# Expert weights in 8 KB rows with ordered features, a twentieth place by shared buffers, and the token gather over four PSUM banks

## The chip, the cores and the metric

The kernel runs on one core of one Trainium2 chip, in one launch. The metric is the device time of one execution in microseconds. Before the change it is 1816.79 us, the median of three runs (1816.61 to 1819.65).

## The reference

Everything is computed in fp32. A sequence of 256 tokens of width 1024 (with 16 meta tokens ahead of it in the first part) passes two layers of a first block and then one hybrid layer, whose second half is a mixture of experts. Cut to what matters here:

```
def swiglu(x, w_gate, w_up, w_down):
    return (silu(x @ w_gate) * (x @ w_up)) @ w_down

def first_block(...):                      # 272 x 1024, two layers
    h = h + 0.5 * swiglu(rmsnorm(h), ...)  # inner width 2816
    proj = rmsnorm(h) @ w_in               # retention and differential attention
    h = h + concat([y_ret, y_diff]) @ w_out
    h = h + 0.5 * swiglu(rmsnorm(h), ...)

def hybrid_layer(...):                     # 256 x 1024, modulated by c
    x = x + g1 * (concat([chunk_mlp, attention, hgrn]) @ w_out)
    h2 = rms(x) * norm2_w * (1.0 + sc2) + sh2
    x = x + g2 * hier_moe(h2, ...)

def hier_moe(h, ...):                      # 4 groups of 8 experts, 32 in all
    grp = argmax(h @ w_grp + b_grp)        # each token: one group,
    top_val, top_idx = top_k(e_in, 2)      # then the best 2 of its 8 experts
    gate = softmax(top_val) * p_grp
    out[e] = (silu(xb @ w1[e]) * (xb @ w3[e])) @ w2[e]     # inner width 512
    y = segment_sum(out * gate, token)
```

## The kernel before

The first block and the hybrid layer's mixer take the first 1317 us of the span. The rest is the mixture of experts: a routing stage (`route`), then 16 pairs of experts, one after the other (`pairs`), which begin at about 1336 us. The change lies in these two, but for one small addition in the stage that computes the modulation.

The routing stage normalizes the tokens, computes the logits, picks group and experts, and numbers the tokens of each expert (`place`). Its ACT writes `h2`, the tokens scaled by their norm, with the tokens on the partitions (L1636).

A pair works on 64 slots for each of its two experts, 128 columns in all. Its steps are:

- `picked` (DVE, L1726): two 0/1 matrices `pick` that say which token sits in which slot.
- `tokens`, the gather: for each of the 8 chunks k of 128 features, two matmuls `xgp` (L1738, one for each half of the tokens) of `h2` with `pick`; then an eviction `xg` that applies the norm's weight and the modulation, for even k by ACT (L1744), for odd k by DVE (L1742). The PSUM tiles alternate between the tags "tp" and "po", one bank each.
- `first` (L1767): `ph` = 32 matmuls with the first weight, into one bank, then 32 with the third into another. Each has 64 slots of one expert as the stationary side and 512 columns of the weight as the moving one.
- Silu by ACT (L1508) of the first `ph` into `h`; the product with the second `ph` by DVE (L1512).
- `turned` (four transposes `hTp`, L1773) and `turned_out`, in which ACT copies one half of `hTp` (L1779) and DVE the other (L1780) to `hTe`.
- `last` (L1787): `py`, one tile of two banks (tag "sc"), 16 matmuls for columns 0 to 511 and 16 for 512 to 1023. Behind each half `weighed` follows: `y` = gate x modulation x `py` (DVE, L1795), `yh` = `y` rounded to the matmul's format (ACT, L1796), `yl` = the rest (DVE, L1797).
- `combine`: `po` (L1805, four matmuls per half) adds the pair's result to the tokens' rows, `xtok` (DVE, L1807). It is done one pair later, between the steps of the next pair. `slots` (`pgt`, L1751 and L1755) prepares the transposed matrix and the gates for it.

The program's order on TensorE is written out by hand in this phase (each matmul is pinned behind the one before): the 64 `ph` of pair g, the gather of pair g+1, `hTp` of pair g, `po` of pair g-1, `py`, and so on. The other engines' order follows from a scheduler. Waits are set by tiles: an instruction that writes a tile waits for the earlier readers of that tile's buffer.

After pair 6 the program asks whether an expert has more than 64 tokens (`overflow`, L1561); the results so far are added first, without other work between. The branch is not taken with these inputs.

Weights come by SP's queue (`load`, L1822), in pieces of 1 MB, 12 for a pair: per expert two of the first weight, two of the third (each 512 rows) and two of the second (each 512 columns). A piece has 128 partitions with four rows of 512 values each, so 2 KB lie together in DRAM. The pieces go round a ring of 19 places, most of which are buffers that earlier stages no longer need; MW = 2 of them are the expert phase's own. A piece is fetched as soon as the matmuls of the piece that held its place are done. The last pair's pieces come in smaller parts.

Of the kernel before, what the change touches and what calls it, by code (L numbers as in the profile page):

```python
# [18 lines left out]
P = 128  # L19
D = 1024  # L20
# [126 lines left out]

CUTS = {True: ((0, 256, 512), (0, 256, 512)), False: ((0, 512), (0, 512))}
ORD = (((0, 1, 6, 7),), ((2, 3), (4,), (5,)))
OVERFLOW = 7  # L150
MW = 2
CONSTS = [
# [14 lines left out]
def _pf_layout():  # L167
    o = 0
    for name, n in (("f1n0", 8), ("f1n1", 8), ("mxn0", 8), ("mxn1", 8), ("f2n0", 8), ("f2n1", 8),
                    ("fin", 8), ("n1w", 8), ("gn0", 4), ("gn1", 4), ("sub0", 1), ("sub1", 1),  # L170
                    ("c", 8), ("cctx", 8), ("hgw", 1), ("n2w", 8)):
        PF[name] = (o, n)
        o += n
    return o
# [5 lines left out]
class Kernel:  # L180
# [633 lines left out]
    def modulation(self):  # L814
# [6 lines left out]
        self.mcol = self.cp.tile([P, 4, KC], F32, name="mcol")  # L821
        self.m2col = self.cp.tile([P, 2, KC], F32, name="m2col")
        self.mrow = self.dp.tile([8, 1, D], F32, name="mrow")
        for part in range(6):
# [17 lines left out]
            for i in range(1 + both):  # L842
                hl = self.gp.tile([P, 2, D], F32R, name="mhl", tag="gb")
                for q in range(0, D, 256):
                    qs = slice(q, q + 256)
                    nc.scalar.activation(hl[:, 0, qs], acc[:, i, qs], AF.Copy)
                    nc.gpsimd.tensor_tensor(hl[:, 1, qs], acc[:, i, qs], hl[:, 0, qs].bitcast(F32), op=ALU.subtract)
                    if q % 512:
                        yield
                yield  # L850
                yield
                row = acc[0:1, i]
                for h in range(2):
# [6 lines left out]
                nc.scalar.dma_start(mrow, row)  # L860
                if part not in (2, 5):
# [12 lines left out]
        o = PF["n2w"][0]  # L874
        nc.vector.scalar_tensor_tensor(self.rc, self.rc, 1.0, self.pf[:, o:o + KC], op0=ALU.add, op1=ALU.mult)
        cst = self.cp.tile([P, 64 + 36 + P], F32, name="cst")
        nc.scalar.dma_start(cst, A["rcst"])
# [609 lines left out]
    def pairs(self):  # L1487
# [9 lines left out]
        for g in range(NPAIR):  # L1497
# [48 lines left out]
            for n in range(2):  # L1546
                for c in (slice(a, b) for a, b in zip(CUTS[True][n], CUTS[True][n][1:])):
                    self.last(py, hT, ws[4 + n], cur, n, c)
                    due.append(slice(512 * n + c.start, 512 * n + c.stop))
# [4 lines left out]
    def overflow(self):  # L1554
# [6 lines left out]
        with tc.If(nc.values_load(self.most[0:1, 0:1], min_val=0, max_val=SEQ) > CAP,  # L1561
                   preferred_fallthrough_block=False):
            with tc.For_i(0, NPAIR, 1) as iv:
# [3 lines left out]
                for r in range(1, SEQ // CAP):  # L1567
# [6 lines left out]
                    w = self.weights(src, ring, eng=nc.gpsimd)  # L1574
                    h = self.late.tile([P, 512], F32, name="h", tag="h", bufs=1)
                    for i in range(2):
# [3 lines left out]
                        if i:  # L1580
                            nc.vector.tensor_tensor(h, h, ps, op=ALU.mult)
                        else:
                            nc.scalar.activation(h, ps, AF.Silu)
                    hT = self.turned_out(self.turned(h))
                    self.outputs(cur)
                    py = self.ps.tile([P, 2, 512], F32, name="py", tag="sc", bufs=1)
                    for n in range(2):
                        self.last(py, hT, next(w), cur, n, slice(0, 512))
                        self.combine(cur, slice(512 * n, 512 * n + 512))
# [5 lines left out]
    def route(self):  # L1595
# [3 lines left out]

        before = ep.tile([P, P], F32R, name="before")  # L1600
        nc.vector.tensor_copy(before, self.before)
# [3 lines left out]
        for tt in range(2):  # L1605
            xT = sm.tile([P, KC, P], F32, name="x2T", tag="xg", bufs=2)
            for q in range(2):
# [26 lines left out]
        for tt in range(2):  # L1634
            r = ss[:, tt, 4:5]
            nc.scalar.activation(self.h2[:, tt], self.xtok[:, tt], AF.Copy, scale=r)  # L1636
        cnt = [0]

        def t(*dims):
            cnt[0] += 1  # L1640
            return sm.tile([P, 2] + list(dims), F32, name="r%d" % cnt[0], tag="r%d" % cnt[0], bufs=1)

# [71 lines left out]
    def picked(self, e0, r=0, place=None, room=None):  # L1714

        nc, sm = self.nc, self.sm
        if place is None:
            place = self.place[:, :, e0:e0 + 2]
        pick = sm.tile([P, 2, P], F32, name="pick", tag="pick", bufs=2) if room is None else room[:, KC:]
        for tt in range(2):  # L1720
            pl = place[:, tt]
            if r:
# [5 lines left out]
                                    self.iota[:, None, :].to_broadcast([P, 2, CAP]), op=ALU.is_equal)  # L1728
        xg = sm.tile([P, KC, P], F32, name="xg", tag="xg", bufs=2) if room is None else room
        return {"pick": pick, "xg": xg}  # L1730

    def tokens(self, cur, ks):

        nc = self.nc
        for k in ks:
            ps = self.pbank("xgp", ("tp", "po")[k % 2])
            for tt in range(2):
                self.pin(nc.tensor.matmul(ps[:, :P], self.h2[:, tt, k * P:k * P + P], cur["pick"][:, tt],  # L1738
                                          start=tt == 0, stop=tt == 1))
            o, sc, sh = cur["xg"][:, k], self.rc[:, k:k + 1], self.sh2[:, k:k + 1]  # L1740
            if k % 2:
# [21 lines left out]
    def first(self, ps, cur, w, kk):  # L1763
        for k in range(4):
            for j in range(2):
                hj = slice(CAP * j, CAP * j + CAP)
                self.pin(self.nc.tensor.matmul(ps[hj], cur["xg"][:, 4 * kk + k, hj], w[j][:, k], start=kk + k == 0,  # L1767
                                               stop=kk == 1 and k == 3))

    def turned(self, h):  # L1770
        pt = self.pbank("hTp", "ot")
        for f in range(4):
            self.pin(self.nc.tensor.transpose(pt[:, f * P:(f + 1) * P], h[:, f * P:(f + 1) * P], self.ident))  # L1773
        return pt
# [7 lines left out]

    def last(self, py, hT, w, cur, n, c):
# [4 lines left out]
        self.weighed(py, cur, n, c)  # L1788
# [22 lines left out]

    def load(self, aps, ring, row, col, rows=(0, 4), cols=(0, 512), eng=None):

        ws = []
        for ap in aps:
            pool, tag, bufs = ring.pop(0)
            ring.append((pool, tag, bufs))
            ws.append(pool.tile([P, 4, 512], F32, name="ew", tag=tag, bufs=bufs))
        for k0, k1 in zip(rows, rows[1:]):
            for a, b in zip(cols, cols[1:]):  # L1820
                for w, ap in zip(ws, aps):
                    (eng or self.nc.sync).dma_start(w[:, k0:k1, a:b], ap[row + k0 * P:row + k1 * P, col + a:col + b]  # L1822
                                                    .rearrange("(k p) f -> p k f", p=P))
        return ws

    def weights(self, src, ring, end=False, eng=None):

        for i in range(2):
            for kk in range(2):
                yield self.load([s[i] for s in src], ring, kk * 512, 0, (0, 2, 4) if end else (0, 4), eng=eng)  # L1830
        for n in range(2):
            yield self.load([s[2] for s in src], ring, 0, n * 512, cols=CUTS[end][n], eng=eng)

# [12 lines left out]
def host_arrays(inputs):  # L1846
# [4 lines left out]
    for n in ("ffn1_w_gate", "ffn1_w_up", "ffn1_w_down", "w_in", "w_out", "ffn2_w_gate", "ffn2_w_up",  # L1851
# [7 lines left out]
             "hgw": np.concatenate([g["hgrn_norm_w_2"][0], g["hgrn_norm_w_2"][0]]), "n2w": g["norm2_w_2"][0]}  # L1859
    f["pf"] = np.concatenate([cols(parts[n]) for n in PF], axis=1)  # L1860
    lv = np.stack([g["diff_lambda_q1"], g["diff_lambda_q2"], g["diff_lambda_k1"], g["diff_lambda_k2"]], axis=1)
# [29 lines left out]
```

## Time and profile before

| | us |
|---|---|
| median of three runs | 1816.79 |
| lowest, highest | 1816.61, 1819.65 |
| the profiled execution's own time | 1815.69 |
| its span, first to last instruction | 1814.0 |
| TensorE busy | 1757.8 (97%) |
| DVE busy, ACT busy | 1035.4, 737.1 |

The profile is of one execution, 1.7 us longer than its span and 1.1 us shorter than the median. Engines are PE (TensorE), PEld (its weight loads, which overlap with matmuls), DVE, ACT, POOL and SP, whose queue (SPq) issues transfers. A row of a timeline gives start, duration, engine, line and operation, "out<-in" by the names of the program, the partitions x elements, and in brackets how long the engine stood idle before it and what ended that. Lines (L1738) are those of the kernel before.

### The profile page before, as it was taken

How to read it: one execution, taken by the hardware profiler on the slowest of the kernel's cores; microseconds unless marked ns; L12 is line 12 of the kernel's file. 1: busy time of each engine (PE TensorE's matmuls, PEld its weight loads, DVE VectorE, ACT ScalarE, POOL GpSimd, SP SyncE). 2: the span in 40 equal slices, each digit the busy share in tenths (PEclk: the TensorE clock that was granted, in tenths of full speed). 3: DMA queues.
4: the chain of work that ended last, by engine and by line, in shares of the span. 5: the costliest groups of instructions: out<-in, count | busy, mean ns of one | idle time of the engine just before them, and what ended most of it. 6: DMA issues, size and time to landing. Idle time of an engine off the chain costs nothing. (4 is left out here: it accounts for less than half of the span.)

```text
span 1814.0 us, 30657 instructions
## 1 busy us (share of the span) xinstructions
PE 1757.8 (97%) x12435; PEld 1439.5 (79%) x12435; DVE 1035.4 (57%) x1764; ACT 737.1 (41%) x1312; POOL 343.8 (19%) x341
## 2 busy tenths in 40 slices
PE   9999999999999999999999999999989999899998
PEld 8999988899999999999899999986654444344444
DVE  6875887676667667668677755648332323122323
ACT  6444445454444544444455544656421111111111
POOL 3231273121221213236131102311000000000000
PEclk9999999999999999999999999999989999899999
DMA  8766643255677576754355655431789999999998
GB/s 253 231 209 192 227 163 117 70 171 166 206 232 247 174 249 211 232 189 133 114 172 170 187 190 164 160 123 41 248 315 380 397 400 400 397 400 400 399 398 306
DMA packets 312946, 427.75 MB, mean 236 GB/s; under 512 B 15056, under 2 KB 207312, under 8 KB 312672
## 3 DMA queue, kind: packets, MB, share of 16 engines
q1 hardware_dynamic: 294640, 394.51, 63.1%
q10 hardware_dynamic: 18160, 31.23, 5.2%
q8 instruction: 100, 1.64, 0.4%
q14 instruction: 46, 0.38, 0.1%
HBM read 424.56 MB, written 1.15 MB: 235 GB/s over the span
## 5 line engine op out<-in xcount | busy, mean ns | idle before, releaser
L265 DVE TENSOR_TENSOR whl<-raw,whl 128x1024 fp32r<-128x1024 f32 (+2 forms) x374 | 464.4, 1246 | 208.5 <-ACT whl L264 207.5
L264 ACT ACTIVATE whl<-raw 128x1024 fp32r<-128x1024 f32 (+2 forms) x374 | 383.8, 1032 | 331.2 <-PE pd L275 107.9
L273 PE MATMUL pgu<-xh,whl 128*128 128x272 f32 (+1 forms) x1408 | 403.8, 287 | 3.6 <-DVE g L348 3.3
L275 PE MATMUL pgu<-xh,whl 128*128 128x272 f32 (+1 forms) x1408 | 403.1, 286 | 2.4 <-DVE whl L265 2.4
L274 PE MATMUL pgu<-xl,whl 128*128 128x272 f32 (+1 forms) x1408 | 402.9, 286 | 1.4 <-DVE xl L286 1.4
L273 PEld LDWEIGHTS pgu<-xh,whl 128*128 128x128 f32 x1408 | 264.1, 188 | 5.5 <-issue 3.5
L275 PEld LDWEIGHTS pgu<-xh,whl 128*128 128x128 f32 x1408 | 265.0, 188 | 3.2 <-DVE whl L265 3.0
L274 PEld LDWEIGHTS pgu<-xl,whl 128*128 128x128 f32 x1408 | 265.1, 188 | 2.3 <-DVE xl L286 2.0
L1767 PE MATMUL ph<-ew,xg 128*64 128x512 f32 x1024 | 225.4, 597 | 6.8 <-issue 6.8
L275 PE MATMUL pd<-ah,whl 128*128 128x272 f32 (+1 forms) x704 | 203.2, 289 | 0.3 <-DVE whl L265 0.3
L274 PE MATMUL pd<-al,whl 128*128 128x272 f32 (+1 forms) x704 | 202.4, 288 | 0.0
L273 PE MATMUL pd<-ah,whl 128*128 128x272 f32 (+1 forms) x704 | 202.3, 287 | 0.0
L1767 PEld LDWEIGHTS ph<-ew,xg 128*64 128x64 f32 x1024 | 74.1, 138 | 152.0 <-issue 148.3
L352 POOL TENSOR_TENSOR u<-u,g 128x272 f32<-128x272 f32 (+1 forms) x88 | 92.1, 1047 | 397.1 <-DVE u L351 339.9
L273 PEld LDWEIGHTS pd<-ah,whl 128*128 128x128 f32 x704 | 132.9, 189 | 0.5 <-issue 0.2
L273 PE MATMUL pj<-xh,whl 128*128 128x272 f32 x448 | 133.2, 298 | 0.0
L275 PEld LDWEIGHTS pd<-ah,whl 128*128 128x128 f32 x704 | 132.5, 188 | 0.6 <-DVE whl L265 0.5
L274 PEld LDWEIGHTS pd<-al,whl 128*128 128x128 f32 x704 | 132.8, 189 | 0.1
L274 PE MATMUL pj<-xl,whl 128*128 128x272 f32 x448 | 130.5, 291 | 0.5 <-DVE xl L286 0.5
L275 PE MATMUL pj<-xh,whl 128*128 128x272 f32 x448 | 130.1, 290 | 0.0
L1787 PE MATMUL py<-ew,hTe 128*64 128x512 f32 (+1 forms) x544 | 117.4, 573 | 2.1 <-ACT hTe L1779 1.0
L1512 DVE TENSOR_TENSOR h<-h,ph 128x512 f32<-128x512 f32 x16 | 11.0, 687 | 175.6 <-PE ph L1767 175.6
(442 smaller groups left out, 2733.2 us busy)
## 6 DMA issues: line engine op xcount, KB each, us to landing
ew<-in_w_dram SPq DMA_DIRECT2D x180, 1024.0 KB, 13.8
raw<-in_ffn_w_gate_dram SPq DMA_DIRECT2D x43, 1024.0 KB, 5.5
raw<-in_ffn_w_up_dram SPq DMA_DIRECT2D x43, 1024.0 KB, 5.6
raw<-in_w_in_dram SPq DMA_DIRECT2D x38, 1024.0 KB, 5.1
raw<-in_ffn_w_down_dram SPq DMA_DIRECT2D x32, 1024.0 KB, 6.2
mraw<-in_w_mod_dram ACTq DMA_DIRECT2D x24, 1024.0 KB, 6.0
raw<-in_ffn_w_down_dram SPq DMA_DIRECT2D x16, 768.0 KB, 5.4
ew<-in_w_dram SPq DMA_DIRECT2D x24, 512.0 KB, 11.0
```

The costliest lines, as they stand in the source:

```text
L264: nc.scalar.activation(w[:, 0], part, AF.Copy)
L265: nc.vector.tensor_tensor(w[:, 1], part, w[:, 0].bitcast(F32), op=ALU.subtract)
L273: nc.tensor.matmul(out, wh, xh, start=first, stop=False)
L274: nc.tensor.matmul(out, wh, xl, start=False, stop=False)
L275: nc.tensor.matmul(out, wl, xh, start=False, stop=last)
L352: nc.gpsimd.tensor_tensor(u[:, :N], u[:, :N], g[:, :N], op=ALU.mult)
L1512: self.nc.vector.tensor_tensor(h, h, ph, op=ALU.mult)
L1767: self.pin(self.nc.tensor.matmul(ps[hj], cur["xg"][:, 4 * kk + k, hj], w[j][:, k], start=kk + k == 0, stop=kk == 1 and k == 3))
L1787: self.pin(self.nc.tensor.matmul(py[hj, n, c], hT[:, k, hj], w[j][:, k, c], start=k == 0, stop=k == 3))
```

## The change

Four things are done. (a) A piece is laid so that a partition holds consecutive rows of the weight: 4 rows of 512 values of the first and third weight, or 2 rows of 1024 values of the second, 8 KB in one stretch. Rows p*8+k of the first two now lie on partition p, so the features are gathered in that order: `h2` is written permuted (ACT, with a stride on both sides), the norm's weight and modulation are loaded a second time in that order (`n2e`, `m2e`), Silu writes `h` permuted (`by_row`) and the product reads `ph` with a stride of four values. (b) The ring gets a twentieth place (MW = 3). `pick` and `xg` have one buffer each where they had two, `y` shares the buffer of `h`, and the temporaries of the routing stage use buffers that the expert phase needs later. (c) As a piece of the second weight now has 256 inner rows and all 1024 columns, `last` does the first two inner chunks for both halves of `py`, then the other two; both `weighed` follow behind. The last pair keeps the old way (`last_part`). (d) The gather uses four banks: chunks with k % 4 below 2 a tile `ps` of two banks under the tag "sc" (which `py` uses as well), the others "tp" and "po".

```
-MW = 2
+MW = 3
...
-            h = self.late.tile([P, 512], F32, name="h", tag="h", bufs=1)
-            self.nc.scalar.activation(h, ph, AF.Silu)
+            h = self.late.tile([P, 4, P], F32, name="h", tag="h", bufs=1)
+            self.nc.scalar.activation(self.by_row(h), ph, AF.Silu)
...
-            self.nc.vector.tensor_tensor(h, h, ph, op=ALU.mult)
+            self.nc.vector.tensor_tensor(h, h, ph.rearrange("p (q k) -> p k q", k=4), op=ALU.mult)
...
-                self.last(py, hT, ws[4], cur, 0, slice(0, 512))
+                self.last(py, hT, ws[4], 0)
...
-                self.last(py, hT, ws[5], cur, 1, slice(0, 512))
+                self.last(py, hT, ws[5], 1)
+                for n in range(2):
+                    self.weighed(py, cur, n, slice(0, 512))
...
-            self.nc.scalar.activation(self.h2[:, tt], self.xtok[:, tt], AF.Copy, scale=r)
+            self.nc.scalar.activation(self.h2[:, tt].rearrange("p (k q) -> p k q", k=KC),
+                                 self.xtok[:, tt].rearrange("p (q k) -> p k q", k=KC), AF.Copy, scale=r)
...
-        pick = sm.tile([P, 2, P], F32, name="pick", tag="pick", bufs=2) if room is None else room[:, KC:]
+        pick = sm.tile([P, 2, P], F32, name="pick", tag="pick", bufs=1) if room is None else room[:, KC:]
...
-        xg = sm.tile([P, KC, P], F32, name="xg", tag="xg", bufs=2) if room is None else room
+        xg = sm.tile([P, KC, P], F32, name="xg", tag="xg", bufs=1) if room is None else room
...
     def tokens(self, cur, ks):
+        if "ps" not in cur:
+            cur["ps"] = self.ps.tile([P, 2, 512], F32, name="xgp", tag="sc", bufs=1)
         for k in ks:
-            ps = self.pbank("xgp", ("tp", "po")[k % 2])
+            ps = cur["ps"][:, k % 4, :] if k % 4 < 2 else self.pbank("xgp", ("tp", "po")[k % 2])
...
-            o, sc, sh = cur["xg"][:, k], self.rc[:, k:k + 1], self.sh2[:, k:k + 1]
+            o, sc, sh = cur["xg"][:, k], self.rce[:, k:k + 1], self.she[:, k:k + 1]
...
+    def last(self, py, hT, w, kk):
+        for k in range(2):
+            for n in range(2):
+                for j in range(2):
+                    hj = slice(CAP * j, CAP * j + CAP)
+                    self.pin(self.nc.tensor.matmul(py[hj, n], hT[:, 2 * kk + k, hj], w[j][:, k, n * 512:n * 512 + 512],
+                                                   start=2 * kk + k == 0, stop=2 * kk + k == 3))
...
-        y = self.late.tile([P, 512], F32, name="y", tag="y", bufs=1)[:, :c.stop - c.start]
+        y = self.late.tile([P, 512], F32, name="y", tag="h", bufs=1)[:, :c.stop - c.start]
...
+        for r, c in cuts:
+            for w, ap in zip(ws, aps):
+                ap = ap.rearrange("(p k) f -> p k f", p=P)
+                (eng or self.nc.sync).dma_start(w[:, r, c], ap[:, rows, cols][:, r, c])
```

The two engines of the gather, as the built programs have them. First TensorE (PE), the gather between two pairs, before; "waits Activation_49" is a wait for ACT's semaphore, "waits DVE_49" for DVE's, and a row with xN stands for N alike:

```order
L1738 MATMUL xgp<-pick,h_14530 128x128 x4
L1738 MATMUL xgp<-pick,h_14530 128x128 [waits Activation_49]
L1738 MATMUL xgp<-pick,h_14530 128x128
L1738 MATMUL xgp<-pick,h_14530 128x128 [waits DVE_49]
L1738 MATMUL xgp<-pick,h_14530 128x128
L1738 MATMUL xgp<-pick,h_14530 128x128 [waits Activation_49]
```

The same place on TensorE now, the whole gather with what stands ahead of and behind it (two matmuls are a chunk):

```order
L1787 MATMUL ph_15030<-ew,xg 64x512 x6
L1758 MATMUL xgp<-pick,h_14534 128x128 [waits DVE_49,PE_49]
L1758 MATMUL xgp<-pick,h_14534 128x128
L1758 MATMUL xgp<-pick,h_14534 128x128 [waits Activation_49]
L1758 MATMUL xgp<-pick,h_14534 128x128 x5
L1758 MATMUL xgp<-pick,h_14534 128x128 [waits DVE_49]
L1758 MATMUL xgp<-pick,h_14534 128x128
L1758 MATMUL xgp<-pick,h_14534 128x128 [waits Activation_49]
L1758 MATMUL xgp<-pick,h_14534 128x128 x3
L1758 MATMUL xgp<-pick,h_14534 128x128 [waits DVE_49]
L1758 MATMUL xgp<-pick,h_14534 128x128
L1797 MATMUL hTp<-ident,h 128x128 x4
```

Before, every chunk from the third on waits for the eviction of two chunks ahead. Now chunk 1 (third matmul) and chunk 5 wait for ACT, chunks 4 and 7 for DVE, and chunks 2, 3 and 6 have no wait of their own.

DVE at the overflow check, from the last pair ahead of it to the branch, before:

```order
L1807 TENSOR_TENSOR xtok<-xtok,po 128x512 [waits PE_49] x2
L1795 SCALAR_TENSOR_TENSOR y<-py,gs,g2row 128x512 [waits DVE_49,PE_49]
L1807 TENSOR_TENSOR xtok<-xtok,po 128x512 [waits PE_49] x2
L1797 TENSOR_TENSOR yl<-y,yh 128x512 [waits Activation_49]
L1795 SCALAR_TENSOR_TENSOR y<-py,gs,g2row 128x512 [waits DVE_49,PE_49]
L1807 TENSOR_TENSOR xtok<-xtok,po 128x512 [waits PE_49] x2
```

And now, with the load of the check's value:

```order
L1840 TENSOR_TENSOR xtok<-xtok,po 128x512 [waits PE_49] x4
L1828 SCALAR_TENSOR_TENSOR y<-py,gs,g2row 128x512 [waits DVE_49,PE_49]
L1830 TENSOR_TENSOR yl<-y,yh 128x512 [waits Activation_49]
L1828 SCALAR_TENSOR_TENSOR y<-py,gs,g2row 128x512 [waits DVE_49]
L1840 TENSOR_TENSOR xtok<-xtok,po 128x512 [waits PE_49] x2
L1830 TENSOR_TENSOR yl<-y,yh 128x512 [waits Activation_49]
L1571 TENSOR_LOAD mi [waits DVE_49]
```

The first `y` and its `yl` have moved behind the last `py`, next to the second `y`; two `xtok` additions stand between the second `y` and its `yl`, in both.

## Rows read from the trace of the kernel before

**Rows 1.** The head of the page: span; busy time of the engines.

```profile
span 1814.0 us, 30657 instructions
PE 1757.8 (97%) x12435; PEld 1439.5 (79%) x12435; DVE 1035.4 (57%) x1764; ACT 737.1 (41%) x1312; POOL 343.8 (19%) x341
```

**Rows 2.** A stretch of one pair: busy us by engine, clock, DMA share, GB/s.

```profile
1395.95:1424.65 28.70, 28.39 (x152) 12.81 (x150) 8.33 (x16) 4.52 (x10) 0.00 (x0) 1.00 1.05 403
```

**Rows 3.** The chain of waits through one pair: start, duration, what.

```profile
1609.34 13.73 PE ph L1767 x64
1623.07 0.66 PE xgp L1738 x4
...
1623.75 0.47 ACT xg L1744
...
1624.26 0.73 PE xgp L1738 x4
...
1638.06 13.73 PE ph L1767 x64
```

**Rows 4.** Waits of the weight loads, expert phase: total us, times, longest.

```profile
PEld xgp L1738 <- ACT xg L1744: 13.3, 45, 0.4
...
PEld ph L1767 <- DMA ew<-in_w_dram: 3.4, 12, 0.3
```

**Rows 5.** The timeline of one gather.

```profile
1409.78 0.97 PEld L1738 LDWEIGHTS xgp<-pick,h 128*128 128x128 f32 x8 [0.81 <-issue]
...
1410.00 0.69 DVE L1512 TENSOR_TENSOR h<-h,ph 128x512 f32<-128x512 f32 x1 [11.60 <-PE ph L1767]
1410.54 0.46 ACT L1744 ACTIVATE xg<-xgp,m2col 128x128 f32<-128x128 f32 x1 [6.88 <-PE xgp L1738]
...
1411.04 0.97 PEld L1738 LDWEIGHTS xgp<-pick,h 128*128 128x128 f32 x8 [0.29 <-ACT xg L1744]
1411.80 0.46 ACT L1744 ACTIVATE xg<-xgp,m2col 128x128 f32<-128x128 f32 x1 [0.80 <-PE xgp L1738]
...
1412.30 0.97 PEld L1738 LDWEIGHTS xgp<-pick,h 128*128 128x128 f32 x8 [0.29 <-ACT xg L1744]
...
1413.56 0.97 PEld L1738 LDWEIGHTS xgp<-pick,h 128*128 128x128 f32 x8 [0.29 <-ACT xg L1744]
...
1414.45 0.47 PEld L1773 LDWEIGHTS hTp<-ident,h 128*128 128x128 f32 x4
```

**Rows 6.** Who waited for the two copies of `hTp`: us, times.

```profile
  DVE hTe L1780: 7.5, 15
```

**Rows 7.** The timeline from the last `py` half of pair 6 to the check.

```profile
1535.57 0.20 PEld L1787 LDWEIGHTS py<-ew,hTe 128*64 128x64 f32 x4 [0.36 <-DVE y L1795]
...
1539.30 0.75 DVE L1795 SCALAR_TENSOR_TENSOR y<-py,gs,g2row 128x512 f32<-128x512 f32 x1 [2.16 <-PE py L1787]
...
1539.96 1.27 DVE L1807 TENSOR_TENSOR xtok<-xtok,po 128x512 f32<-128x512 f32 x2
...
1542.46 0.40 PE L1805 MATMUL po<-yl,pT 128*128 128x512 f32 x1
```

**Rows 8.** The timeline from a second `y` to the next Silu.

```profile
1424.90 0.75 DVE L1795 SCALAR_TENSOR_TENSOR y<-py,gs,g2row 128x512 f32<-128x512 f32 x1 [2.21 <-PE py L1787]
...
1426.41 0.69 DVE L1797 TENSOR_TENSOR yl<-y,yh 128x512 fp32r<-128x512 f32 x1 [0.76 <-ACT yh L1796]
...
1431.77 0.60 ACT L1508 ACTIVATE h<-ph 128x512 f32<-128x512 f32 x1 [5.39 <-PE ph L1767]
```

**Rows 9.** DMA queue of SP, 1400:1500 us: packets, MB, share of 16 engines.

```profile
q1 hardware_dynamic: 20034, 39.78, 104.6%
```

**Rows 10.** The same queue in 1133.4:1137.1 us, a load with 8 KB rows.

```profile
q1 hardware_dynamic: 144, 1.05, 82.4%
```

**Rows 11.** ACT's timeline in the routing stage, at `h2`.

```profile
1323.35 2.17 ACT L1636 ACTIVATE h<-xtok,ss 128x1024 f32<-128x1024 f32 x2
1327.60 0.21 ACT L1688 ACTIVATE r<-r 128x8 f32<-128x8 f32 x1 [2.08 <-POOL r L1687]
```

More of the change, by code (lines that the diff above doesn't have):

```diff
@@ L146 @@
 CAP = 64
-CUTS = {True: ((0, 256, 512), (0, 256, 512)), False: ((0, 512), (0, 512))}
+CUTS = ((0, 256, 512), (0, 256, 512))
 ORD = (((0, 1, 6, 7),), ((2, 3), (4,), (5,)))
 OVERFLOW = 7
-MW = 2
+MW = 3
 CONSTS = [
@@ L822, in modulation @@
         self.m2col = self.cp.tile([P, 2, KC], F32, name="m2col")
+        self.m2e = self.cp.tile([P, 2, KC], F32, name="m2e")
         self.mrow = self.dp.tile([8, 1, D], F32, name="mrow")
@@ L860, in modulation @@
                 nc.scalar.dma_start(mrow, row)
+                if part in (3, 4):
+                    nc.scalar.dma_start(self.m2e[:, part - 3], mrow.rearrange("o (p k) -> p (o k)", p=P))
                 if part not in (2, 5):
@@ L1546, in pairs @@
             for n in range(2):
-                for c in (slice(a, b) for a, b in zip(CUTS[True][n], CUTS[True][n][1:])):
-                    self.last(py, hT, ws[4 + n], cur, n, c)
+                for c in (slice(a, b) for a, b in zip(CUTS[n], CUTS[n][1:])):
+                    self.last_part(py, hT, ws[4 + n], n, c)
+                    self.weighed(py, cur, n, c)
                     due.append(slice(512 * n + c.start, 512 * n + c.stop))
@@ L1574, in overflow @@
                     w = self.weights(src, ring, eng=nc.gpsimd)
-                    h = self.late.tile([P, 512], F32, name="h", tag="h", bufs=1)
+                    h = self.late.tile([P, 4, P], F32, name="h", tag="h", bufs=1)
                     for i in range(2):
@@ L1580, in overflow @@
                         if i:
-                            nc.vector.tensor_tensor(h, h, ps, op=ALU.mult)
+                            nc.vector.tensor_tensor(h, h, ps.rearrange("p (q k) -> p k q", k=4), op=ALU.mult)
                         else:
-                            nc.scalar.activation(h, ps, AF.Silu)
+                            nc.scalar.activation(self.by_row(h), ps, AF.Silu)
                     hT = self.turned_out(self.turned(h))
@@ L1587, in overflow @@
                     for n in range(2):
-                        self.last(py, hT, next(w), cur, n, slice(0, 512))
+                        self.last(py, hT, next(w), n)
+                    for n in range(2):
+                        self.weighed(py, cur, n, slice(0, 512))
                         self.combine(cur, slice(512 * n, 512 * n + 512))
@@ L1598, in route @@
         rev = self.rev
-        before = ep.tile([P, P], F32R, name="before")
+        before = self.late.tile([P, P], F32R, name="before", tag="hTe", bufs=1)
         nc.vector.tensor_copy(before, self.before)
@@ L1605, in route @@
         for tt in range(2):
-            xT = sm.tile([P, KC, P], F32, name="x2T", tag="xg", bufs=2)
+            pool, tag = ((sm, "xg"), (self.late, "yh"))[tt]
+            xT = pool.tile([P, KC, P], F32, name="x2T", tag=tag, bufs=1)
             for q in range(2):
@@ L1635, in route @@
             r = ss[:, tt, 4:5]
-            nc.scalar.activation(self.h2[:, tt], self.xtok[:, tt], AF.Copy, scale=r)
-        cnt = [0]
+            nc.scalar.activation(self.h2[:, tt].rearrange("p (k q) -> p k q", k=KC),
+                                 self.xtok[:, tt].rearrange("p (q k) -> p k q", k=KC), AF.Copy, scale=r)
+        room = self.late.tile([P, 1024], F32, name="rt", tag="yl", bufs=1)
+        at = [0]
         def t(*dims):
-            cnt[0] += 1
-            return sm.tile([P, 2] + list(dims), F32, name="r%d" % cnt[0], tag="r%d" % cnt[0], bufs=1)
+            n = 2 * int(np.prod(dims))
+            at[0] += n
+            r = room[:, at[0] - n:at[0]]
+            return r.rearrange("p (a b c) -> p a b c", a=2, b=dims[0]) if len(dims) > 1 else r.rearrange("p (a b) -> p a b", a=2)
         tt_, pool = nc.vector.tensor_tensor, nc.gpsimd.tensor_tensor
@@ L1768, in first, with by_row @@
                                                stop=kk == 1 and k == 3))
+    def by_row(self, h):
+        return h.rearrange("p k q -> p q k")
     def turned(self, h):
@@ L1781, in turned_out, with last_part @@
         return hT
-    def last(self, py, hT, w, cur, n, c):
+    def last(self, py, hT, w, kk):
+        for k in range(2):
+            for n in range(2):
+                for j in range(2):
+                    hj = slice(CAP * j, CAP * j + CAP)
+                    self.pin(self.nc.tensor.matmul(py[hj, n], hT[:, 2 * kk + k, hj], w[j][:, k, n * 512:n * 512 + 512],
+                                                   start=2 * kk + k == 0, stop=2 * kk + k == 3))
+    def last_part(self, py, hT, w, n, c):
         for k in range(4):
@@ L1810, in combine, with load @@
                 eng.dma_start(self.A["out"][0, tt * P:(tt + 1) * P, ns], self.xtok[:, tt, ns])
-    def load(self, aps, ring, row, col, rows=(0, 4), cols=(0, 512), eng=None):
+    def load(self, aps, ring, rows, cols, cuts, eng=None):
         ws = []
@@ L1817, in load @@
             ring.append((pool, tag, bufs))
[L1818 to L1823, printed above, removed]
+            w = pool.tile([P, 4, 512], F32, name="ew", tag=tag, bufs=bufs)
+            n, f = rows.stop - rows.start, cols.stop - cols.start
+            ws.append(w.rearrange("p a b -> p (a b)").rearrange("p (a b) -> p a b", a=n, b=f))
+        for r, c in cuts:
+            for w, ap in zip(ws, aps):
+                ap = ap.rearrange("(p k) f -> p k f", p=P)
+                (eng or self.nc.sync).dma_start(w[:, r, c], ap[:, rows, cols][:, r, c])
         return ws
     def weights(self, src, ring, end=False, eng=None):
+        every = slice(None)
         for i in range(2):
             for kk in range(2):
-                yield self.load([s[i] for s in src], ring, kk * 512, 0, (0, 2, 4) if end else (0, 4), eng=eng)
+                yield self.load([s[i] for s in src], ring, slice(4 * kk, 4 * kk + 4), slice(0, 512),
+                                [(slice(0, 2), every), (slice(2, 4), every)] if end else [(every, every)], eng)
         for n in range(2):
-            yield self.load([s[2] for s in src], ring, 0, n * 512, cols=CUTS[end][n], eng=eng)
+            if end:
+                yield self.load([s[2] for s in src], ring, slice(0, 4), slice(512 * n, 512 * n + 512),
+                                [(every, slice(a, b)) for a, b in zip(CUTS[n], CUTS[n][1:])], eng)
+            else:
+                yield self.load([s[2] for s in src], ring, slice(2 * n, 2 * n + 2), slice(0, D), [(every, every)], eng)
 def body(tc, A, stop=None, skip1=False):
@@ L1859, in host_arrays @@
              "hgw": np.concatenate([g["hgrn_norm_w_2"][0], g["hgrn_norm_w_2"][0]]), "n2w": g["norm2_w_2"][0]}
-    f["pf"] = np.concatenate([cols(parts[n]) for n in PF], axis=1)
+    f["pf"] = np.concatenate([cols(parts[n]) for n in PF if n != "n2e"] + [g["norm2_w_2"][0].reshape(P, KC)], axis=1)
     lv = np.stack([g["diff_lambda_q1"], g["diff_lambda_q2"], g["diff_lambda_k1"], g["diff_lambda_k2"]], axis=1)
```

8 lines of the change are left out of this document (5 added, 3 removed).

## Prediction

> **What bounds the kernel now.** I read four views, in this order. The head of the page gives a span of 1814.0 us with TensorE busy for 97% of it [rows 1], so only time that TensorE waits or works can be saved or added. All parts of the change lie in the expert phase or in the routing stage ahead of it; I therefore looked at the phase in stretches of one pair of experts. One such stretch of 28.70 us has TensorE busy for 28.39 us at a granted clock of 1.00, while the transfers run at 403 GB/s and over their own full share (1.05) [rows 2]. Both look like the bound, and the third view decides: the chain of waits through a later pair goes from one 64-fold `ph` group to the next in 1638.06 - 1609.34 = 28.72 us, and it holds TensorE work and ACT's gather evictions (0.47 us each), no transfer [rows 3]. The waits say the same: TensorE's weight loads wait for an expert piece 12 times, 0.3 us at most, 3.4 us in all, and for ACT's `xg` 45 times, 13.3 us in all [rows 4]. The transfers run ahead by the ring of places, and TensorE sets the pace. Yet 12 pieces of 1.05 MB at 39.78 MB in 100 us [rows 9] take 31.6 us, more than a pair of TensorE: that lag is paid out of the ring's lead, and the chain shows none of it surface.
>
> The fourth view is the timeline of one gather, the only place in a pair where TensorE stands still for another engine. Before, chunk k uses one bank, "tp" for even k and "po" for odd k. Weight loads of even chunks begin at 1409.78, 1411.04, 1412.30, 1413.56 [rows 5]: 1.26 us from one to the next, because chunk k+2 needs the bank that ACT empties (matmuls of two chunks, then 0.46 us of ACT, then the release). The last two chunks wait for nothing behind them: 1414.45 - 1413.56 = 0.89 us, so a chunk that need not wait costs 0.445 us. The gather is 3 x 1.26 + 0.89 = 4.67 us.
>
> **The gather in four banks (the term that decides).** By its shape the change gives each chunk a bank that was left four chunks ago. But two of the four banks are one tile "ps" of two banks, and the program waits for a tile, not for a bank. In the order of the changed kernel (shown under the change) chunk 1 waits for ACT, which empties chunk 0 out of the same tile; chunk 4 waits for DVE (chunk 1), chunk 5 again for ACT (chunk 4). Chunks 2, 3 and 6 wait for nothing new, and chunk 7's wait for DVE's chunk 3 is long over. That a tile is waited for as a whole is no guess: before, the two halves of `hTp`, which two engines copy out, go one after the other (DVE's `hTe` waited for ACT's 15 times, 7.5 us [rows 6]), and `py` for columns 512 to 1023, in its second bank, waited for DVE's `y` out of the first (weight load at 1535.57, 0.36 us behind DVE `y` [rows 7]).
>
> What a wait for ACT costs is in rows 5. It was 1.26 us for two chunks; for the chunk just ahead, the path is the chunk's two matmuls until ACT can start (1409.78 to 1410.54, 0.76), the eviction (0.46), and the release (0.04): again 1.26, now for one chunk. So the new gather is: chunk 0 to 1, 1.26; 1 to 4, 3 x 0.445 = 1.335; 4 to 5, 1.26 (chunk 4's own wait for DVE is hidden: chunk 1 is ready 0.76 after its load, DVE needs some 0.4, and three chunks take 1.335); 5 to the end, 1.335. Sum 5.19 us against 4.67: +0.52 us. The bounds: below, 8 x 0.445 = 3.56 us, -1.11, if the halves of the tile don't hold each other up; above, +0.9, if DVE's chunk 1 delays chunk 4 as well by about one eviction. I take +0.52, as the rows and the order together give it. Times 15 gathers between pairs: **+7.8 us** (-16.6 to +13.5). The first gather is done in two halves of four chunks: before 1.26 + 0.89 = 2.15, after 1.26 + 1.335 = 2.6, twice +0.44: **+0.9 us**.
>
> The Trainium skill (Perfetto Trace Analysis, section Optimizing Tensor Performance, Matmuls) says that independent groups should rotate through different PSUM banks so that evictions overlap the next matmuls. Rows 5 agree where the banks alternate: two chunks go by for one eviction. Taken for the four banks here it would give the lower end, 3.56 us a gather; it speaks of banks, and the order of this program holds back by tiles.
>
> **`last` in the order kk, and `weighed` behind it.** Before, the first half's `y`, `yh`, `yl` ran beside the second half's matmuls. Now both run after the last matmul: `y` to the end of `yl` is 1424.90 to 1427.10, 2.20 us [rows 8], twice that 4.4 us. Its cover is the next pair's 32 `ph` matmuls until Silu needs the shared buffer "h" at 1431.77, 6.9 us behind the first `y`: 2.5 us to spare, so nothing, 14 times. The matmuls are as many as before.
>
> It has no cover once: at the overflow check after pair 6, where `po` follows at once. Before, `po` ended at 1542.46 + 0.40 = 1542.86, 3.56 us behind the start of the one `y` still to do at 1539.30 [rows 7]. Now two chains stand there, and DVE has two `xtok` additions (1.27 us, rows 7) between the second `y` and its `yl`: `y` 1539.30, first `yl` ends 1541.5, second `y` 1542.25, `xtok` to 1543.6, second `yl` 1544.3, `po` of the second half about 1545.3: **+2.4 us**. Bounds: 0 (if DVE got through first) to one whole chain and both additions, 3.5.
>
> **8 KB pieces, 20 places.** The lag of the transfers is 31.6 - 28.7 = 2.9 us a pair, 46 us over 16 pairs; 19 places hold 19 x 1.05 MB / 398 GB/s = 50 us. So some 4 us are to spare at the end, the twentieth place adds 2.6, and a TensorE that is 8 us slower adds as much: 15 us. What 8 KB packets cost, before shows only in one short transfer: 144 packets, 1.05 MB, 82.4% of the engines for 3.7 us [rows 10], which is 1.05 / (3.7 x 0.824) = 344 GB/s at a full share; the stream of 2 KB packets has 39.78 MB / (100 us x 1.046) = 380. Slower by 10% would be 50 us more lag, less the 15 to spare: +35 us. Faster by any amount saves nothing, since at most 3.4 us were ever waited for. I take 0: the 2 KB row is a long stream, the other the start of a single transfer beside others, so its share is the less certain of the two; +35 stays as the upper end of rival C.
>
> The Trainium skill (DMA: Bandwidth & Descriptors, section Why small descriptors are slow) names a fixed cost per packet that long ones spread. By it the pieces come sooner than rows 9 have them, and the term is 0 for certain; no row of before shows such a gain.
>
> **Strided operands and single buffers.** Silu writes and the product reads with a stride; the product took 0.69 us at 1410.00 and `hTp` needs it only at 1414.45, and DVE's chunk 1 comes at about 1411.8, so it may double for nothing; at four times (2.8 us) it would delay chunk 1's eviction, and by it chunk 4, by about 0.9 us per pair. h2 in the new order is two ACT instructions of together 2.17 us with 2.08 us free behind them [rows 11]: nothing up to a doubling. One `pick` and one `xg` buffer instead of two: `pick` is rewritten after the gates' matmuls, `xg` after the last `ph`, both over by the next use. I take 0 for all, with -1 to +1 for the routing stage.
>
> **Sum.** 7.8 + 0.9 + 2.4 = +11.1 us. The profiled execution took 1815.69, 1.7 us over its span and 1.1 below the median of 1816.79: 1826.8 by the one, 1827.9 by the other. I say **1827.5**.
>
> **Rivals.** (B) The four banks turn freely, by whatever means the program lets them: 15 x -1.11 and 2 x (4 x 0.445 - 2.15 = -0.37) are -17.4, with +2.4 for the check -15.0: 1802.5. Then the transfers would lag by 2.9 + 1.1 = 4.0 us a pair, 64 us, where 20 places hold 52.6: without faster packets up to 11 us of it would be lost, 1813.5. For it: ACT is idle for 0.80 us ahead of the eviction at 1411.80 [rows 5], so a dependency and no lack of time makes the pattern; against it: the waits of the order and rows 6 and 7. It decides from the point where chunk 1 starts 0.45 us behind chunk 0. Chance 0.07. (C) The strides or the long packets cost: a product at four times its time adds 15 x 0.9 = 13.5, packets slower by 10% up to 35: 1838 to 1862. For it: no row of before shows such strides, and the one of such packets is slow; against it: some 3 us of slack per pair for the one, 15 us for the other. Chance 0.1. (D) Only one of the two waits of a gather holds TensorE, because the other's eviction is over when its chunk comes: 5.19 - (1.26 - 0.445) = 4.375 us, -0.3 a gather and -4.4 in all, which the other two terms (+3.3) take back: -1.1, no change, 1815.7. For it: chunk 5 has the longer row of evictions behind it, so ACT may be done; against it: ACT can't start on chunk 4 before its matmuls end, 0.76 us behind its load. Chance 0.08. The forecast, 1823 to 1833: 0.75.
>
> A measurement of this kernel can tell 0.2% (3.6 us) from no change. Slower: 0.75 + 0.1 = 0.85; within: D, 0.08; faster: B, 0.07. For 8 in 10 the range runs from 1817 (a little above D) to 1837 (where C starts).
>
> **What would show it.** Silu starts 29.2 us apart instead of 28.7; in the gather two gaps of about 0.8 us behind ACT's `xg`, ahead of chunks 1 and 5, none ahead of 3 or 7; weight loads of `ph` still wait for no piece; after pair 6 two `y` chains before `po`. Wrong, if Silu starts 27.6 apart (B), if `ph` waits for pieces (C), or if DVE's product takes over 2 us.

## The result and the profile after

The changed kernel takes 1829.88 us (median of 4 runs, 1821.92 to 1830.56) against 1817.22 us: 1.006 times the kernel before, 95% interval 1.0043 to 1.0078. Timed once more beside other kernels it was 1825.59 us (11 runs) against 1817.70: 1.0056 (1.0035 to 1.0077). So it is slower by 0.6%, some 10 us, as forecast. The profiled execution took 1821.92 us, 6.2 more than the one before.

The head of the page after (span; busy time of the engines) answers to [rows 1]: TensorE isn't busier, it waits longer.

```profile
span 1820.2 us, 30659 instructions
...
PE 1755.0 (96%) x12435; PEld 1439.9 (79%) x12435; DVE 1039.2 (57%) x1765; ACT 748.1 (41%) x1312; POOL 341.8 (19%) x341
```

The timeline of one gather after, chunk 0 to the transposes, answers to [rows 5]. Columns as there.

```profile
1438.84 0.52 PEld L1758 LDWEIGHTS xgp<-pick,h 128*128 128x128 f32 x4 [0.81 <-issue]
...
1439.05 0.69 DVE L1519 TENSOR_TENSOR h<-h,ph 128x512 f32<-128x512 f32 x1 [9.49 <-PE ph L1787]
1439.59 0.46 ACT L1764 ACTIVATE xg<-xgp,m2e 128x128 f32<-128x128 f32 x1 [6.40 <-PE xgp L1758]
1440.10 1.86 PEld L1758 LDWEIGHTS xgp<-pick,h 128*128 128x128 f32 x16 [0.74 <-ACT xg L1764]
...
1440.93 0.41 DVE L1762 TENSOR_SCALAR xg<-xgp,m2e 128x128 f32<-128x128 f32 x1 [1.19 <-PE xgp L1758]
...
1442.19 0.46 ACT L1764 ACTIVATE xg<-xgp,m2e 128x128 f32<-128x128 f32 x1 [0.43 <-DVE xg L1762]
1442.70 1.41 PEld L1758 LDWEIGHTS xgp<-pick,h 128*128 128x128 f32 x12 [0.74 <-ACT xg L1764]
...
1444.04 0.47 PEld L1797 LDWEIGHTS hTp<-ident,h 128*128 128x128 f32 x4
```

There are two gaps of 0.74 us behind ACT's `xg`, ahead of chunk 1 and chunk 5, and none ahead of the others: 1444.04 - 1438.84 = 5.20 us, where the forecast had 5.19. Chunk 5 shows best that it is the tile that counts, not the bank. Its own bank was chunk 1's, and DVE had emptied that by 1440.93 + 0.41 = 1441.34; chunk 5's turn came at 1440.10 + 4 x 0.445 = 1441.88. Yet it waited until 1442.70, just behind ACT's eviction of chunk 4 out of the other bank (1442.19 + 0.46 = 1442.65). The profile names DVE's `xg` as what ended ACT's idle time at 1442.19. ACT began 0.75 us behind the turn of chunk 4, as it did behind chunk 0's (1438.84 to 1439.59), so it waited for its own matmuls at least as long; that the evictions hold each other up isn't shown.

The waits of the weight loads in the whole phase (us, times, longest) answer to [rows 4]:

```profile
PEld xgp L1758 <- ACT xg L1764: 22.3, 30, 0.8
...
PEld ph L1787 <- DMA ew<-in_w_dram: 0.9, 3, 0.3
```

Fewer waits (from 1350 us on 30 against 45 [rows 4]), each some two and a half times as long; pieces are waited for even less than before.

Silu's starts, a pair apart, and with them its duration (before 0.60 us [rows 8]):

```profile
1432.12 1.07 ACT L1515 ACTIVATE h<-ph 128x512 f32<-128x512 f32 x1 [3.27 <-PE ph L1787]
1461.36 1.07 ACT L1515 ACTIVATE h<-ph 128x512 f32<-128x512 f32 x1 [3.27 <-PE ph L1787]
```

The pair takes 29.24 us, +0.52. The strided write costs ACT 0.47 us more, and `h2` 2.13 us an instruction where it was half of 2.17 [rows 11]; the product with a stride in PSUM takes 0.69 us as before. None of these is waited for.

SP's queue in 1400:1500 us, 8 KB rows (packets, MB, share), answers to [rows 9]:

```profile
q1 hardware_dynamic: 5767, 41.97, 101.0%
```

41.97 MB where it was 39.78: the stream with 8 KB rows is 5% faster, the opposite of what [rows 10] gave.

After pair 6 (weight loads left out, but for the last row; SP's row is where the next pieces are issued):

```profile
1541.79 0.75 DVE L1828 SCALAR_TENSOR_TENSOR y<-py,gs,g2row 128x512 f32<-128x512 f32 x1 [2.81 <-PE py L1813]
...
1545.82 0.69 DVE L1830 TENSOR_TENSOR yl<-y,yh 128x512 fp32r<-128x512 f32 x1
...
1547.58 0.63 PE L1838 MATMUL po<-yl,pT 128*128 128x512 f32 x1
...
1549.16 13.26 SPq L1858 DMA_DIRECT2D ew<-in_w_dram  x8
1552.28 0.32 PEld L1787 LDWEIGHTS ph<-ew,xg 128*64 128x64 f32 x4 [4.79 <-issue]
1552.31 9.29 PE L1787 MATMUL ph<-ew,xg 128*64 128x512 f32 x32 [4.10 <-issue]
```

From the `y` that follows the last `py` to the end of `po` it is 6.42 us where it was 3.56 [rows 7]: +2.86. Some 0.7 us of that is the clock: from the last wait for `yl` to the end, `po` took 1.65 us at a granted clock of 0.51 (nearly all at the lower of its two levels, 1.2 GHz), where before it took 0.97 at 1.00 (2.4 GHz). But behind the branch TensorE then stood idle for 4.10 us, where before it was 6.79; I call this time the stand. That gave nearly all of it back, and I hadn't foreseen it. The row of before:

```profile
1549.64 9.32 PE L1767 MATMUL ph<-ew,xg 128*64 128x512 f32 x32 [6.79 <-issue]
```

**Where the time went.** Profiles of kernels that are alike up to the routing stage begin it anywhere from 1314.3 to 1321.6 us (dips of the granted clock in the first 1310 us fall differently: 0.95 to 1.00 in the first 100 us). I therefore compare from the first `x2p` of that stage to the end of the span: before 1814.0 - 1317.2 = 496.8, after 1820.2 - 1316.1 = 504.1 and, in the second profile, 1823.8 - 1319.5 = 504.3. So the stage lost 7.3 to 7.5 us by these profiles. The true loss is some 0.6 us more, since the profile of before has a dip of the clock within the stage. Its `lg` matmuls ran at a granted clock of 0.50, those of the changed kernel at 1.00, before and after:

```profile
1322.77 3.63 PE L1614 MATMUL lg<-wr,x2T 128*128 128x36 f32 x16
1320.54 1.98 PE L1627 MATMUL lg<-wr,x2T 128*128 128x36 f32 x16 [0.25 <-ACT x2T L1625]
```

Experiments 6 and 10 are the kernel before up to the Silu of pair 0 and have no such dip there: from the first `x2p` to that Silu they take 29.4 us, the profile of before 29.9.

The rest of the difference of the medians, at most 5 us, goes with the clock too. The 15 timed executions of the changed kernel fall nearly in the order of their mean granted clock: 1822 us at 0.991, 1825.6 at 0.988, 1828.3 to 1830.6 at 0.986 and below, and one of 1844.93 at 0.937. At the same mean clock the changed kernel is 9 to 10 us slower than the one before (at 0.988 on average 1825.6 against 1816.8, at 0.986 1829.5 against 1819.5). Why the clock falls differently from one execution to the next, and where the longest ones lose their time, stays open: none of them was profiled.

### The profile page after: what moved, and what is told of

It reads as the page before. It is cut to its first block, busy times and chain, and to the rows that moved or that the text cites. A ratio compares the mean times of both kernels' runs of the same rounds, so it can differ in the third digit from the quotient of the medians.

```text
span 1820.2 us, 30659 instructions
## 1 busy us (share of the span) xinstructions
PE 1755.0 (96%) x12435; PEld 1439.9 (79%) x12435; DVE 1039.2 (57%) x1765; ACT 748.1 (41%) x1312; POOL 341.8 (19%) x341
## 5 line engine op out<-in xcount | busy, mean ns | idle before, releaser
L1813 PE MATMUL py<-ew,hTe 128*64 128x512 f32 x480 | 109.3, 597 | 0.9 <-ACT hTe L1803 0.9
```

Source lines behind the costliest of these rows:

```text
L1813: self.pin(self.nc.tensor.matmul(py[hj, n], hT[:, 2 * kk + k, hj], w[j][:, k, n * 512:n * 512 + 512], start=2 * kk + k == 0, stop=2 * kk + ...
```

## Experiments

Each kernel is the changed one or the one before with the edit shown. "Stage" is the time from the first `x2p` to the end, in its profile.

**1. The changed kernel again** (no edit).

> The changed kernel once more, timed in five rounds beside the kernel before. Theory: pairs 29.24 us apart against 28.72 because chunks 1 and 5 of the gather wait for ACT, so 6 to 13 us slower than before. What is open is why its single executions lie between 1821.9 and 1830.6 us: if the granted clock goes with it (0.990 at 1821.9, 0.985 at 1830), the longer executions have a stretch at the lower clock in one place, with pairs as long as in the shorter ones; if the transfers do it, weight loads of ph wait for pieces in the longer ones.

1825.59 us, 1.0056 (1.0035 to 1.0077); stage 504.3. Pairs 29.24 apart and the same waits. Its profiled execution began the routing stage 3.4 us later than the first profile's and had the same stage: these two executions differ ahead of the change, not in it. Of the two explanations expected for the scatter the mean clock goes with the times, as told above; pieces are waited for no more in this profile than in the first (1.1 us in all).

**2. Four tiles: neighbouring chunks never in one tile.**

```
         for k in ks:
-            ps = cur["ps"][:, k % 4, :] if k % 4 < 2 else self.pbank("xgp", ("tp", "po")[k % 2])
+            if k % 4 == 0:
+                ps = cur["ps"][:, k // 4, :]
+            elif k % 4 == 1:
+                ps = self.mm("xgp")
+            else:
+                ps = self.pbank("xgp", ("tp", "po")[k % 2])
```

> The changed kernel with the gather over four banks that are four tiles (chunk 0 and 4 in the two banks of sc, 1 and 5 in a third bank of the ph tag, the others as before). Theory (the tile is waited for as a whole): a gather takes 8 x 0.445 = 3.56 us instead of 5.20, pairs 27.6 us apart, 15 x 1.64 + 2 x 0.82 = 26 us faster than the changed kernel, about 14 us faster than before, if the transfers keep up (12 pieces at 421 GB/s are 29.9 us a pair, 37 us of lag against 20 places that hold 50). Rival (ACT's and DVE's evictions themselves set the pace): gather stays over 4.6 us and the time is no better than before. Rival (transfers bind once TensorE is quicker): ph waits for pieces late in the phase and at least 10 of the 26 us are lost.

1800.08 us, 0.9904 (0.9889 to 0.9918); stage 480.4. Its gather:

```profile
1437.23 3.65 PEld L1763 LDWEIGHTS xgp<-pick,h 128*128 128x128 f32 x32 [0.81 <-issue]
...
1440.79 0.48 PEld L1802 LDWEIGHTS hTp<-ident,h 128*128 128x128 f32 x4
```

3.56 us without a gap, to the hundredth what [rows 5] gave for chunks that wait for nothing; pairs 27.62 apart to the end of the phase. The edit isn't only another cut of the same four banks: chunks 0 and 4 have the two banks of "sc", 1 and 5 two buffers of the tag of `ph` (three by turns), so this gather goes over six banks. That two banks more were needed is an untested rival; against it stands chunk 5 above, whose own bank was free 0.54 us ahead of its turn. The first rival on record falls: evictions keep up; so does the second: weight loads of `ph` wait 2.6 us in all.

**3. The changed kernel with the two banks of before** (`ps = self.pbank("xgp", ("tp", "po")[k % 2])`).

> The changed kernel with the gather of before (two banks by turns); pieces, places, order of last and all else as changed. Theory: pairs 28.72 us apart again, 15 x 0.53 + 0.9 = 9 us faster than the changed kernel, and what is left against before is the check after pair 6 (+2.4) and nothing else: 1817 to 1821. Rival (strides, single buffers or 8 KB packets cost): it stays 5 us or more above before.

1814.57 us, 0.9991 (0.9982 to 1.0000); stage 494.7, 2.1 us less than before, of which some 0.6 is the dip in the profile of before. The pairs are as expected, 28.72 apart; the time misses the expected 1817 to 1821, chiefly as the stand is 3.8 us, not 6.8:

```profile
1402.69 1.08 ACT L1515 ACTIVATE h<-ph 128x512 f32<-128x512 f32 x1 [3.27 <-PE ph L1785]
1431.40 1.07 ACT L1515 ACTIVATE h<-ph 128x512 f32<-128x512 f32 x1 [3.27 <-PE ph L1785]
```

So strides, single buffers, order of `last` and 8 KB rows cost nothing a pair. Putting the gather back brings 504.3 - 494.7 = 9.6 us; 1.1 of that is not the gather but the check (against the first profile of the changed kernel, a stand of 3.83 us instead of 4.10, and 8.50 us instead of 9.29 for the 32 `ph` behind it, at a mean granted clock of 0.83 instead of 0.76).

**4. The kernel before with four tiles** (the edit of 2 in place of its line).

> The kernel before with nothing changed but the gather over four tiles. TensorE alone would be 15 x 1.11 + 2 x 0.37 = 17.4 us faster: 1799. Theory: 2 KB packets and 19 places then bind: the lag is 31.6 - 27.6 = 4.0 us a pair, 64 us over 16 pairs against 50 that the ring holds, so some 13 of the 17 us are lost: 1808 to 1815, with ph waiting for pieces in the last third of the phase. Rival (the transfers speed up when the places are free earlier): 1799 to 1802 and no such wait.

1815.07 us, 0.9988 (0.9979 to 0.9997). The pairs are 27.61 apart up to the eleventh, and then the transfers set the pace; Silu's starts:

```profile
1633.34 0.60 ACT L1508 ACTIVATE h<-ph 128x512 f32<-128x512 f32 x1 [5.39 <-PE ph L1774]
1660.95 0.60 ACT L1508 ACTIVATE h<-ph 128x512 f32<-128x512 f32 x1 [5.39 <-PE ph L1774]
1689.94 0.60 ACT L1508 ACTIVATE h<-ph 128x512 f32<-128x512 f32 x1 [5.85 <-PE ph L1774]
1721.54 0.60 ACT L1508 ACTIVATE h<-ph 128x512 f32<-128x512 f32 x1 [5.61 <-PE ph L1774]
```

29.0 and 31.6 us, and then 32.57 and 30.95: about the 31.6 that rows 9 gave for 12 pieces. Of the 17 us that TensorE should have saved, 15 were lost so.

**5. The kernel before with only the tile of two banks** (the gather as in the change).

> The kernel before with nothing changed but the gather's banks as in the change (chunks with k % 4 below 2 in one tile of two banks). Theory (the tile is waited for as a whole): a gather takes 5.20 us instead of 4.67, pairs 29.25 us apart instead of 28.72, 15 x 0.53 + 0.9 = 9 us slower: 1826 to 1827, with two waits for ACT of about 0.8 us in each gather. Rival (the loss comes from the strides or the order of last): no slower than before by more than 2 us.

1827.39 us, 1.0059 (1.0046 to 1.0073); stage 504.9. The waits:

```profile
PEld xgp L1740 <- ACT xg L1746: 23.0, 31, 0.8
```

This one edit, alone, costs as much as the whole change: 8.1 us in the stage.

**6 and 7. The check elsewhere**: before with `OVERFLOW = 1`, four tiles with `OVERFLOW = 4`.

> The kernel before with the overflow check after pair 0 instead of after pair 6, where SP has issued the pieces long before and the transfers stand still. TensorE stood 6.8 us behind the branch where weights were moving (before, and 6.4 to 6.5 with four tiles) and 3.8 to 4.3 us where they were idle (the changed kernel, and it with two banks). Theory (what the engines need behind the branch comes through the same DMA engines, behind the weights): the stand behind the branch falls to about 4 us. Rival (the stand goes with the program's size or with the order of the instructions ahead of it): it stays at 6.4 to 6.8 us. The time itself: the transfers lose some 5 us of their lead at the check, of which about 4 are spare, so -3 to +3 us.

> The changed kernel with four tiles, and the check after pair 3 instead of after pair 6: there SP is done with its pieces about 18 us ahead of the branch instead of 11, longer than the 14 us that a piece takes to land, so no weights move at the branch. Theory (the code behind the branch waits behind weights): the stand behind the branch is about 4 us instead of 6.4, and the time 2 to 3 us less than with the check after pair 6 (1800.1), as the lead suffices: 1797 to 1798.5. Rival (program size or order): 6.4 us and 1800.

1825.48 us (1.0048, 1.0034 to 1.0061) and 1799.65 (0.9911, 0.9897 to 0.9924). Both miss on the stand, 6.3 and 5.8 us, and neither tells the theories apart: the transfers moved weights while TensorE stood in both (407 GB/s from 1446 to 1462 us in the second). In the second the profile puts the wait down to a piece, and not to the branch alone:

```profile
PE ph L1792 <- DMA ew<-in_w_dram: 5.8, 1, 5.8
```

Both miss on the time as well. The first was to stay within 3 us of the kernel before and is 8.3 slower: the transfers had stood still for some 5 us ahead of the stand, and the lead lost there came back as pairs of up to 31.6 us at the end. The second was to take 1797 to 1798.5.

**8. Four tiles, 19 places** (`MW = 2`).

> The changed kernel with four tiles and 19 places instead of 20. Theory (8 KB packets, not the twentieth place, keep the transfers ahead): 12 pieces at 421 GB/s take 29.9 us against 27.6 of TensorE, a lag of 37 us over the phase against 50 that 19 places hold, so the pairs stay 27.62 us apart to the end and the time stays at 1799 to 1802. Rival (the twentieth place carries the gain): pairs lengthen late in the phase and some 2.6 us or more are lost.

1800.14 us, 0.9909 (0.9896 to 0.9923), pairs 27.6 apart to the last. The twentieth place brings nothing. What keeps the transfers ahead is then in the rest of the change, and of that the 8 KB rows are what speeds the stream: 42.01 MB in 1400:1500 us, where experiment 4, with 19 places too, has 39.78. No kernel here differs in the rows alone.

**9. Four tiles, four pieces behind the check.**

```
-                    ws = self.loads(g + 1)
+                    src = [tuple(self.A[n][0, 2 * (g + 1) + j] for n in self.names) for j in range(2)]
+                    late = self.weights(src, self.ring)
+                    ws = [next(late) for _ in range(4)]
                     self.overflow()
+                    ws += list(late)
```

> The changed kernel with four tiles, where SP issues the last four of the twelve pieces of the pair after the check behind the check instead of ahead of it. The checks after pair 0 and pair 3 didn't test the stand behind the branch, since weights moved during it in both (6.3 and 5.8 us). Here the transfers are done about 10 us earlier and stand still at the branch. Theory (what the engines need behind the branch comes behind the weights): the stand falls from 6.4 to about 4 us, the time from 1800.1 to about 1797.7, as 37 + 10 us of lag still fit into 52. Rival (program size or order of the instructions): 6.4 us and 1800.

1798.18 us, 0.9893 (0.9877 to 0.9910): the fastest here, 19 us below before, though its interval overlaps with that of 2; its stage is 478.5 us, 1.9 less. The stand:

```profile
PE ph L1795 <- issue: 4.2, 1, 4.2
```

**10. Before, six pieces behind the check** (the edit of 9 with `range(3)`; one execution).

> The kernel before with six of the twelve pieces of the pair after the check held back behind it. Theory: the stand behind the branch falls from 6.8 to about 4 us, if the transfers are then done by the branch; in the end this costs more than it brings, since only some 4 us of lead are spare and up to 15 are given away: pairs lengthen late in the phase. Rival: the stand stays at 6.8 us.

1817.75 us, no difference by a single execution; its stage is 501.8 us, 5 more than before, which an early start of the stage (1314.3 us) hides in the time. By that profile it costs more than it brings, as expected. The stand fell from 6.8, and pairs lengthened at the end:

```profile
PE ph L1770 <- issue: 4.0, 1, 4.0
...
PE ph L1770 <- DMA ew<-in_w_dram: 3.6, 4, 1.6
```

Over twelve profiles the stand is 3.8 to 4.3 us where the weights stood still, or all but, when the branch came (the changed kernel twice, 3, 9, 10), and 5.8 to 6.8 where they moved (before, 2, 4 to 8; 7's is the wait put down to a piece). Holding pieces back, and nothing else, moved two kernels from the one group to the other. In the stand, before and after, one packet of the instruction queue moved; that this packet is what waits behind the weights fits, but no run took it away alone, so it is not shown. The queues before (1543:1550 us) and after (1548:1553 us, with the pieces issued behind the branch):

```profile
q1 hardware_dynamic: 1349, 2.68, 103.7%
q8 instruction: 1, 0.02, 1.0%
...
q1 hardware_dynamic: 109, 0.89, 53.8%
q8 instruction: 1, 0.02, 1.5%
```

## Why the prediction was right, and where it was off

- **The gather**, +7.8 us forecast: right, in mechanism and size. 5.20 us a gather, 15 x 0.53 = 7.9. With the first gather, experiment 5 puts it alone at 8.1 us (8.7 without the dip in before's profile), experiment 3 at 9.6, of which 1.1 lie at the check. The lower bound, 3.56 us, was exact too (experiment 2): it asked for tiles that neighbouring chunks don't share. One row was misread on the way: the 0.36 us at 1535.57 are how long the weight load stood idle until DVE's `y` ended it; `y` had ended 0.23 us before. That `py` waited for `y` holds.
- **The first gather**, +0.9: right in the sum. From the first `x2p` to the Silu of pair 0 it is 30.2 us with the shared tile alone (experiment 5) against 29.4 in experiments 6 and 10: +0.8. Its second half took 2.80 us against 2.35, the 0.45 forecast; the first 4.61 against 3.75, +0.86, since it ran at a granted clock of 0.50, and the 16 `ph` behind it ran faster in return. A stall ahead of it (1.17 us behind ACT's `x2T`) went with the new buffers and brought nothing: the `rk` matmuls came 12.0 us behind the first `x2p`, where they come at 11.8 in experiments 4, 5, 6 and 10.
- **The check**, +2.4: `po` came 2.86 us later, near the 2.4 reckoned, but the step failed in its sum, because the stand behind the branch was left out as if it were constant. It fell by 2.7 us, since SP's pieces were through when the branch came (experiments 9 and 10), and left +0.2.
- **`last` and `weighed` at nothing**: nearly. Pairs 0 and 7, with no pair ahead of them, are 0.3 to 0.5 us shorter in experiment 3 (26.83 against 27.17, 28.07 against 28.52), as `py` no longer waits for `y` between its halves.
- **8 KB rows and the places at nothing**: right here, as TensorE paces both kernels. The bound from [rows 10] had the wrong sign: a short start beside other transfers was no measure of a stream. The lag worked out for rival B (4.0 us a pair, up to 11 us lost with 20 places) is what experiment 4 shows at 2 KB rows and 19 places, where 13 were expected and 15 lost.
- **The sum**: 11.1 us forecast, 7.3 to 7.5 in the stage by two profiles (some 8 without the dip in before's), 7.9 and 12.7 between medians. That the time of 1827.5 lies between the two medians is in part luck: the scatter of the clock made up for the term of the branch.
- **Rivals**: B was not what the program did; with four tiles it became true. C fell: no stride was waited for. D fell: both waits held TensorE. Two of their sums were off: by its own terms B comes to 1816.8 - 15.0 = 1801.8, not 1802.5, and C starts at 1827.5 + 13.5 = 1841, not 1838; neither changes which one the result picks.

The rule of the Trainium skill on banks (Perfetto Trace Analysis, section Optimizing Tensor Performance) holds in experiment 2; the changed kernel shows that banks in one tile don't count as different ones in this program.

## What to carry to other kernels

Count the tiles, not the banks: a buffer over two banks that two engines empty is one thing to wait for, and the waits in the built order show it before any run. Before paying for faster transfers or more places, see which side paces the phase; here the quicker gather brought 2.6 us in the kernel before (experiment 4) and 17.6 with the rest of the change around it (experiment 2), while that rest without it brought some 3 (experiment 3). The time that an engine stands behind a branch isn't a constant: look at what moves on the DMA engines when it comes. Before comparing two profiles, even of one stage, look for dips of the granted clock in it.

## Unexpected on the hardware

ACT slows by the stride of what it writes, 0.60 to 1.07 us for 128x512 and 1.14 to 2.13 us for 128x1024 (there its input is strided too), while DVE's product, reading PSUM at every fourth value, stays at 0.69 us. The stand behind the branch took 3.8 to 4.3 us with idle transfers and 5.8 to 6.8 with weights moving. The mean granted clock differs from one execution of the same kernel to the next, 0.984 to 0.991 in fourteen of fifteen, and the time goes with it, 1830 to 1822 us.
